# A two-layer block with product-key experts on one core: 32 latent tokens moved from dense expert products to row gathers

## The chip, the core and the metric

One core of a Trainium2 chip. TensorE (PE) multiplies, VectorE (DVE) and ScalarE (ACT) work element by element, GpSimd (POOL) issues the indirect DMAs, SyncE (SP) most other DMAs. The metric is the device time of one execution in microseconds (us).

## The reference, cut to what matters

Two layers, each a mixer followed by `peer` on T = 640 tokens of width D = 1024: 128 context tokens and 512 latent ones, which differ only in their modulation. Each token scores 128 x 128 experts by product keys, takes 16 for each of 8 heads, and mixes their rows:

```python
def peer(h, wq, sub_keys, u, v):
    ...
        eidx = jnp.take_along_axis(cidx, fi, axis=-1)
        g = jax.nn.softmax(fs, axis=-1)
        act = jax.nn.gelu(jnp.einsum('cd,chkd->chk', xc, u[eidx]).astype(F32), approximate=False)
        return jnp.einsum('chk,chkd->cd', (g * act).astype(v.dtype), v[eidx])
```

So a token reads 128 rows of `u` and 128 rows of `v` (4 KB each) of the 16384 in each table.

## The kernel before

**Two ways to the experts.** The 512 latent tokens go through all 16384 experts densely. For each i (128 experts), the product `S` is 24 matmuls of 128x512 (high and low halves of `uT` and of the activations, L1130 to L1133), `S_gelu` takes it through gelu, and `w1` (L1478) multiplies it by the gate matrix `gt`, which is zero for experts that a token did not choose. `w1` also casts the high half `Wh` on ACT, and `w2` (L1486) makes the low half `Wl` on DVE. The output product `O` (L1517 to L1521) sums eight i's at a time: 16 chunks `cc`, in each eight products, one per 128 columns `dt` of D, again 24 matmuls each. `evac` (L1527) adds each into the residual `xT`. The 128 context tokens go by gathers: POOL fetches one row per token (128 rows of 4 KB) by an indirect DMA (L1424). DVE takes its dot product with the activations (`gu`, L1431) or adds it, weighted, to `acc` (`gv`, L1440): 256 such steps per layer. Four row buffers serve them.

**Stages of a layer.** After the mixer come the query projection (`pqs`, L1189) and, tile by tile of 128 tokens, scores (`scp`), the top-k chains on DVE (L1236 on) and transposes of the result (`hk`). Groups of eight tokens get one-hot matrices (DVE, L1338 to L1341), whose products `G` (L1352, L1353) are the gate matrix, stored in `Gd`. During this stage, here the ahead stage, PE also makes 72 of the 128 `S` products (list AHEAD) and stores their gelu in `Sd`; DVE makes the low half `ul` of each `uT` block for them (L220). The main stage follows. In each chunk PE makes the chunk's own `S` products (NMAIN: 3 and 4 in turn), while the chunk's other gelus come back by `reload` (L1491). Then come its eight `O` products, beginning with the reloaded i's.

**What orders the work.** Each engine runs its instructions in the order of the program, in which `step` spreads the ahead products, one-hot groups and rows over the top-k chain. Rows of the main stage are run by `run_items`, one after an `S` (not the first of a chunk) and two after each `O`. Whatever is left after `O` number 5 of the last chunk runs there in one go, ahead of `ctx_end`, whose transposes `aT` bring `acc` into the residual. A reloaded gelu and a new gelu share three buffers (`gep`). A buffer comes free when its `w2` is done:

```python
def w2(pw):
    i, ge, Wh = pw
    ...
    nc.vector.tensor_tensor(Wl, ge, Wh.bitcast(F32), op=OP.subtract)
```

Of the kernel before, what the change touches and what calls it, by code (L numbers as in the profile page):

```python
# [38 lines left out]
NMAIN = [3, 4] * 8  # L39
# [13 lines left out]
def _trunk(ctx, tc, nc, I, O, n_phases):  # L53
# [1051 lines left out]
    def peer(l, last_layer):  # L1105
        with ExitStack() as s:
            Gd = dram.tile([16, P, NI, 32], F32, name=f"Gd{l}")
            Sd = dram.tile([len(AHEAD), P, TS], F32, name=f"Sd{l}")
            hp = s.enter_context(tc.tile_pool(reuse_waits="tile", name=f"ph{l}", bufs=1))
            h2h = hp.tile([P, NC, TS], F32R, name=f"h2h{l}")  # L1110
            h2l = hp.tile([P, NC, TS], F32R, name=f"h2l{l}")
            h2p = hp.tile([P, D], F32, name=f"h2p{l}")
            eidx = hp.tile([P, P], I32, name=f"eidx{l}")
            gp = hp.tile([P, P], F32, name=f"gp{l}")
# [9 lines left out]
            def S_mm(i, w):  # L1124
                hi, lo = w[:2]
                ps = pp.tile([P, TS], F32, name=f"S{l}_{i}", tag="S", bufs=2)

                for c in range(NC + 5):
                    if c < NC:
                        nc.tensor.matmul(ps, hi[:, c], h2h[:, c], start=(c == 0), stop=False)  # L1130
                        nc.tensor.matmul(ps, hi[:, c], h2l[:, c], start=False, stop=False)  # L1131
                    if c >= 5:
                        nc.tensor.matmul(ps, lo[:, c - 5], h2h[:, c - 5], start=False, stop=(c == NC + 5 - 1))  # L1133
                return ps

            def S_gelu(i, ps):
                ge = gep.tile([P, TS], F32, name=f"ge{l}_{i}", tag="ge")
                nc.scalar.activation(ge, ps, AF.Gelu)  # L1138
                return ge
# [3 lines left out]
            def S_ahead():  # L1143
# [6 lines left out]
                n_ahead[0] += 1  # L1150

            with ExitStack() as s2:
# [4 lines left out]
                with ExitStack() as s3:  # L1157
# [10 lines left out]
                    ph32 = php.tile([P, NC, TP], F32, name=f"ph32{l}")  # L1168
# [4 lines left out]
                    for c in range(NC):  # L1173
                        xr = tp.tile([P, T], F32, name=f"pxr{l}_{c}", tag="nt", bufs=3)
                        for tr, a, b in TRUNKS:
# [3 lines left out]
                        nc.scalar.activation(h2h[:, c], xr[:, TP:], AF.Identity, bias=m[:, 1:2])  # L1179
                        nc.scalar.activation(ph32[:, c], xr[:, :TP], AF.Identity, bias=m[:, 0:1])  # L1180
                        nc.vector.scalar_tensor_tensor(h2l[:, c], xr[:, TP:], m[:, 1:2], h2h[:, c].bitcast(F32),
                                                       op0=OP.add, op1=OP.subtract)

                    for n in range(NC):
                        wh, wl, raw = ws.pop(n) if n in ws else wload(wp, I["pwq"][l, n], P, "w")
                        ps = ppn.tile([P, 2, 512], F32, name=f"pqs{l}_{n}", tag="b2")
                        for c in range(NC):
                            for k, (a, b) in enumerate(((wh, h2h), (wl, h2h), (wh, h2l))):
                                nc.tensor.matmul(ps[:, 0, :], a[:, c], b[:, c], start=(c == 0 and k == 0),  # L1189
                                                 stop=(c == NC - 1 and k == 2))  # L1190
# [38 lines left out]
                def topk(tt, sc_, step):  # L1229
                    nm = f"{l}_{tt}"  # L1230
                    sv = tp.tile([P, 16, 16], F32, name=f"sv{nm}", tag="sv")
                    si = tp.tile([P, 16, 16], U32, name=f"si{nm}", tag="si")
# [11 lines left out]
                    cand = tp.tile([P, 8, 112], F32, name=f"cand{nm}", tag="cand", bufs=1)  # L1244
# [11 lines left out]
                    for h in range(8):  # L1256
                        step(17 + h)
                        c2 = tp.tile([P, 112], F32, name=f"c2{nm}_{h}", tag="c2", bufs=2)
# [52 lines left out]
                def to_hk(tt, g, ij):  # L1311
                    ts = slice((tt - 1) * P, tt * P)
                    ps = pk.tile([P, 4, P], F32, name=f"hk{l}_{tt}", tag="sp")
                    nc.tensor.transpose(ps[:, 0], ij[:, 0], ident)
                    nc.tensor.transpose(ps[:, 1], ij[:, 1], ident)
                    nc.tensor.transpose(ps[:, 2], g, ident)
                    nc.scalar.copy(iT[:, ts], ps[:, 0])
                    nc.scalar.copy(jT[:, ts], ps[:, 1])
                    g32 = tp.tile([P, P], F32, name=f"g32{l}_{tt}", tag="g32")
                    nc.scalar.activation(g32, ps[:, 2], AF.Copy, scale=GSC)  # L1320
                    nc.vector.tensor_copy(gh[:, ts], g32)
                    nc.vector.tensor_tensor(gl[:, ts], g32, gh[:, ts], op=OP.subtract)
# [3 lines left out]
                def build(grp):  # L1326

                    ts = slice(grp * 8, (grp + 1) * 8)

                    def bc(t):  # L1330
                        return (t[:, ts].rearrange("p (b t) -> p b t", t=2).unsqueeze(2)
                                .to_broadcast([P, 4, P, 2]))
                    io = iota2.unsqueeze(1).to_broadcast([P, 4, P, 2])
                    oj = ohp.tile([P, 4, P, 2], F16, name=f"oj{l}_{grp}", tag="oj")
                    oi = ohp.tile([P, 4, P, 2], F16, name=f"oi{l}_{grp}", tag="oi", bufs=1)
                    o1 = ohp.tile([P, 4, P, 2], F16, name=f"o1{l}_{grp}", tag="o1")
                    o2 = ohp.tile([P, 4, P, 2], F16, name=f"o2{l}_{grp}", tag="o2")
                    nc.vector.tensor_tensor(oj, bc(jT), io, op=OP.is_equal)  # L1338
                    nc.vector.tensor_tensor(oi, bc(iT), io, op=OP.is_equal)
                    nc.vector.tensor_tensor(o1, oi, bc(gh), op=OP.mult)  # L1340
                    nc.vector.tensor_tensor(o2, oi, bc(gl), op=OP.mult)  # L1341
                    return oj, o1, o2

                def place(grp, oj, o1, o2):
                    if grp % 4 == 0:
                        stg[0] = ohp.tile([P, P, 32], F32, name=f"stg{l}_{grp}", tag="stg")
                    for q in range(2):
                        ps = pk.tile([P, 4, P], F32, name=f"G{l}_{grp}_{q}", tag="G", bufs=4)
                        for r in range(4):
                            t = q * 4 + r  # L1350
                            b, h = t // 2, t % 2
                            nc.tensor.matmul(ps[:, r], oj[:, b, :, h], o1[:, b, :, h], start=True, stop=False)  # L1352
                            nc.tensor.matmul(ps[:, r], oj[:, b, :, h], o2[:, b, :, h], start=False, stop=True)  # L1353
# [3 lines left out]
                    if grp % 4 == 3:  # L1357
                        for a, b in ((0, NI),) if grp < 63 else ((0, 8), (8, NI)):
# [16 lines left out]


                done = 0.0
                for tt in range(NT):
                    share = 0.12 if tt < 2 else 0.195

                    def step(x):
                        ahead_to(done + share * x / 30)
                        while len(todo) > 16 - 16 * x / 30:
                            build_next()
                    sc_ = scores(tt)
                    if tt == 0:
# [4 lines left out]
                    if tt == 0:  # L1391
                        nc.vector.tensor_copy(gp, g)
                        nc.vector.tensor_scalar(ij[:, 0], ij[:, 0], float(P), float(l * NI * P), op0=OP.mult,
                                                op1=OP.add)
                        nc.vector.tensor_tensor(eidx, ij[:, 0], ij[:, 1], op=OP.add)
                        ahead_to(done)
                    else:
# [4 lines left out]
                        todo.extend(range((tt - 1) * 16, tt * 16))  # L1402
# [8 lines left out]
            with ExitStack() as s2:  # L1411
# [7 lines left out]
                eidx2 = rp.tile([P, P], I32, name=f"eidx2{l}", tag="eidx2", bufs=1)
                dots = rp.tile([P, P], F32, name=f"dots{l}", tag="dots", bufs=1)  # L1420

                def gather(table, k, nm):
                    r = rp.tile([P, D], F32, name=f"{nm}{l}_{k}", tag="row")
                    nc.gpsimd.indirect_dma_start(  # L1424
                        out=r[:], out_offset=None, in_=I[table],
                        in_offset=bass.IndirectOffsetOnAxis(ap=eidx2[:, k:k + 1], axis=0))
                    return r

                def ctx_u(k):
                    r = next_row()  # L1430
                    nc.vector.tensor_tensor_reduce(r, r, h2p, 1.0, 0.0, OP.mult, OP.add, dots[:, k:k + 1])  # L1431
# [6 lines left out]
                def ctx_v(k):  # L1438
                    r = next_row()
                    nc.vector.scalar_tensor_tensor(acc, r, dots[:, k:k + 1], acc, op0=OP.mult, op1=OP.add)  # L1440
# [5 lines left out]
                def fetch(n):  # L1446

                    while wanted and len(rows) < n:
                        rows.append(gather(*wanted.pop(0)))
# [5 lines left out]
                for k in range(NI + 16):  # L1455
                    if k < NI:
                        items.append(lambda k=k: ctx_u(k))
                        wanted.append(("pu", k, "gu"))
                    if k % 16 == 15 and k < NI:
                        items.append(lambda k=k: ctx_gate(k - 15, k + 1))  # L1460
                    if k >= 16:
                        items.append(lambda k=k: ctx_v(k - 16))
                        wanted.append(("pv", k - 16, "gv"))
# [5 lines left out]
                def g_load(q):  # L1469
                    if q >= NI // 4:  # L1470
                        return
                    gts[q] = Gp.tile([P, 16, 4, 32], F32, name=f"gt{l}_{q}", tag="gt")
# [3 lines left out]
                def w1(i, ge):  # L1476
                    gv = ge.rearrange("p (g t) -> p g t", g=16)
                    nc.vector.tensor_tensor(gv, gv, gts[i // 4][:, :, i % 4, :], op=OP.mult)  # L1478
                    Wh = wpool.tile([P, TS], F32R, name=f"Wh{l}_{i}", tag="Wh")
# [317 lines left out]
```

## Time and profile before

| | |
|---|---|
| time, median of 3 runs | 4041.17 us (4034.7 to 4048.16) |
| profiled execution | 4047.5 us |
| its span | 4045.7 us |
| PE busy | 3960.8 us, 98% |
| DVE busy | 2952.9 us, 73% |
| ACT, POOL busy | 1556.8 us, 38%; 727.1 us, 18% |
| mean granted TensorE clock | 0.987 |

The span is from the first to the last instruction. Each part of the sum is read from one stage, since the busy shares are means over stages. A matmul's recorded duration overlaps that of the next one; its step is a row's stretch divided by the count of matmuls in it.

### The profile page before, as it was taken

To read this page: it belongs to the slowest core of one execution; us is meant where nothing else is said; L and a number is where in the kernel's file an instruction comes from. 1 tells how busy PE (TensorE), PEld (TensorE's weight loads), DVE (VectorE), ACT (ScalarE), POOL (GpSimd) and SP (SyncE) were. 2 spreads that over 40 slices of the span, in tenths; PEclk is the share of its full clock that TensorE was granted. 3 is DMA by queue.
4 is the path that set the end of the run, shared out by engine and by line. 5 is a ranking of instruction groups with operands and counts; after the bars stand their busy time and mean duration, and the time that the engine had idled before them with its cause. 6 is when DMAs were issued, how large, how long until landed. Compare 5 with 4: busy or idle time off the path is not lost.

```text
span 4045.7 us, 57051 instructions
## 1 busy us (share of the span) xinstructions
PE 3960.8 (98%) x21578; PEld 3257.8 (81%) x21578; DVE 2952.9 (73%) x6091; ACT 1556.8 (38%) x2322; POOL 727.1 (18%) x687
## 2 busy tenths in 40 slices
PE   7999999999999999999999999999999999999998
PEld 5957988888788888888889778888888888888887
DVE  5254469997677777787775664799967787777875
ACT  3334334566323323223343553355663223233231
POOL 0000000000233333333200120000003333333432
PEclk9999999999999999999999999999999999999999
DMA  5152234557888888888552002345578888887884
GB/s 184 59 188 68 84 106 141 195 203 253 276 301 295 275 296 288 293 302 276 209 188 103 22 22 84 113 159 193 199 269 283 273 300 281 294 304 274 295 298 166
DMA packets 363929, 850.80 MB, mean 210 GB/s; under 512 B 27859, under 2 KB 172165, under 8 KB 356869
## 3 DMA queue, kind: packets, MB, share of 16 engines
q1 hardware_dynamic: 289012, 576.04, 41.1%
q0 software_dynamic: 74640, 271.10, 19.2%
q8 instruction: 170, 2.79, 0.3%
q14 instruction: 107, 0.87, 0.1%
HBM read 738.12 MB, written 108.92 MB: 209 GB/s over the span
## 4 chain that ended last, share of the span: by engine, by line
PE 60%; issue 14%; DVE 12%; DMA 7%; POOL 4%; ACT 2%; SPq 0%; POOLq 0%; DVEq 0%; ACTq 0%
PE S L1130 6%; PE S L1131 6%; PE S L1133 6%; PE O L1521 6%; PE O L1517 6%; PE O L1518 6%; PE ow L246 4%; DMA gu<-in_pu_dram,eidx 3%; PE pqs L1189 2%; DMA gv<-in_pv_dram,eidx 2%; POOL gv L1424 2%; POOL gu L1424 2%; PE et L246 2%; DVE ul L220 1%; PE ef L444 1%
## 5 line engine op out<-in xcount | busy, mean ns | idle before, releaser
L1130 PE MATMUL S<-h2h,uh 128*128 128x512 f32 x2048 | 812.3, 397 | 9.3 <-ACT ge L1138 5.6
L1517 PE MATMUL O<-Wh,vh 128*128 128x512 f32 x2048 | 798.1, 390 | 7.1 <-ACT Wh L1480 4.8
L1131 PE MATMUL S<-h2l,uh 128*128 128x512 f32 x2048 | 800.3, 391 | 0.0
L1518 PE MATMUL O<-Wh,vl 128*128 128x512 f32 x2048 | 797.2, 389 | 0.0
L1521 PE MATMUL O<-Wl,vh 128*128 128x512 f32 x2048 | 782.1, 390 | 0.0
L1133 PE MATMUL S<-h2h,ul 128*128 128x512 f32 x2048 | 589.3, 389 | 0.0
L219 ACT CAST vh<-v_raw 128x1024 fp32r<-128x1024 f32 x256 | 269.7, 1053 | 803.9 <-PE O L1521 723.8
L1424 POOL DMA_INDIRECT gv<-in_pv_dram,eidx x256 | 360.8, 1409 | 797.3 <-DVE acc L1440 770.6
L1130 PEld LDWEIGHTS S<-h2h,uh 128*128 128x128 f32 x2048 | 386.1, 189 | 94.5 <-ACT uh L219 7.3
L1517 PEld LDWEIGHTS O<-Wh,vh 128*128 128x128 f32 x2048 | 384.6, 188 | 90.5 <-ACT Wh L1480 7.4
L1521 PEld LDWEIGHTS O<-Wl,vh 128*128 128x128 f32 x2048 | 385.2, 188 | 80.3
L220 DVE TENSOR_TENSOR ul<-u_raw,uh 128x1024 fp32r<-128x1024 f32 x256 | 312.9, 1223 | 186.6 <-ACT uh L219 141.6
L1133 PEld LDWEIGHTS S<-h2h,ul 128*128 128x128 f32 x2048 | 384.5, 188 | 80.0
L1518 PEld LDWEIGHTS O<-Wh,vl 128*128 128x128 f32 x2048 | 384.6, 188 | 79.3
L1131 PEld LDWEIGHTS S<-h2l,uh 128*128 128x128 f32 x2048 | 386.3, 189 | 76.8
L1424 POOL DMA_INDIRECT gu<-in_pu_dram,eidx x256 | 317.7, 1241 | 515.8 <-DVE dots L1431 367.7
L219 ACT CAST uh<-u_raw 128x1024 fp32r<-128x1024 f32 x256 | 269.1, 1051 | 343.2 <-PE S L1131 313.6
L220 DVE TENSOR_TENSOR vl<-v_raw,vh 128x1024 fp32r<-128x1024 f32 x256 | 312.6, 1221 | 110.1 <-ACT vh L219 107.3
L1440 DVE SCALAR_TENSOR_TENSOR acc<-gv,dots,acc 128x1024 f32<-128x1024 f32 x256 | 327.9, 1281 | 42.0 <-DMA gv<-in_pv_dram,eidx 41.2
L1431 DVE CUSTOM_DVE_ANT_0 gu<-gu,h2p 128x1024 f32<-128x1024 f32 x256 | 311.6, 1221 | 54.7 <-DMA gu<-in_pu_dram,eidx 54.6
L1355 ACT ACTIVATE stg<-G 128x512 f32<-128x512 f32 x256 | 260.9, 1159 | 0.7 <-PE G L1353 0.7
L1418 POOL MEMSET acc<- 128x1024 f32 x2 | 1.9, 958 | 1366.2 <-DVE oj L1338 784.9
(399 smaller groups left out, 6003.5 us busy)
## 6 DMA issues: line engine op xcount, KB each, us to landing
u_raw<-in_uT_dram SPq DMA_DIRECT2D x256, 512.0 KB
v_raw<-in_vR_dram SPq DMA_DIRECT2D x256, 512.0 KB
gt<-Gd SPq DMA_DIRECT2D x64, 1024.0 KB
Gd<-stg SPq DMA_DIRECT2D x30, 2048.0 KB
adaw<-in_adaw_dram SPq DMA_DIRECT2D x80, 512.0 KB
Sd<-ge SPq DMA_DIRECT2D x144, 256.0 KB
gr<-Sd SPq DMA_DIRECT2D x134, 256.0 KB
w_raw<-in_ow_dram SPq DMA_DIRECT2D x12, 1024.0 KB
```

The lines of the kernel that those rows point to most:

```text
L219: nc.scalar.copy(hi, raw)
L220: nc.vector.tensor_tensor(lo, raw, hi.bitcast(F32), op=OP.subtract)
L1130: nc.tensor.matmul(ps, hi[:, c], h2h[:, c], start=(c == 0), stop=False)
L1131: nc.tensor.matmul(ps, hi[:, c], h2l[:, c], start=False, stop=False)
L1133: nc.tensor.matmul(ps, lo[:, c - 5], h2h[:, c - 5], start=False, stop=(c == NC + 5 - 1))
L1355: nc.scalar.activation(stg[0][:, :, t0:t0 + 4].rearrange("p i t -> p t i"), ps, AF.Copy, scale=1.0 / GSC)
L1424: nc.gpsimd.indirect_dma_start(out=r[:], out_offset=None, in_=I[table], in_offset=bass.IndirectOffsetOnAxis(ap=eidx2[:, k:k + 1], axis=0))
L1431: nc.vector.tensor_tensor_reduce(r, r, h2p, 1.0, 0.0, OP.mult, OP.add, dots[:, k:k + 1])
L1440: nc.vector.scalar_tensor_tensor(acc, r, dots[:, k:k + 1], acc, op0=OP.mult, op1=OP.add)
L1517: nc.tensor.matmul(ps, hi[:, order[y]], Wh, start=(y == 0), stop=False)
L1518: nc.tensor.matmul(ps, lo[:, order[y]], Wh, start=False, stop=False)
L1521: nc.tensor.matmul(ps, hi[:, x], Ws[n // NC * CH + x][1], start=False, stop=(y == CH + lag - 1))
```

## The change

- XN = 32: the last 32 latent tokens leave the dense part, whose products have ND = 480 columns. Each gathers its 128 rows from each table, four experts of 32 tokens to a gather of 128 rows, so 32 more gathers for `u` and 32 for `v` per layer, with planes of their own in `h2p` and `acc`; `aX`, eight small products, sums the four planes at the end.
- EARLY = 28 context `u` rows are gathered and dotted in the ahead stage, through one buffer (`erow`).
- NMAIN: 40 `S` products in the main stage instead of 56, 88 ahead instead of 72. Seven chunks between the first and the last have 3, the other seven 2; the first has 3, the last 2.
- The top-k tiles go in the order 0, 4, 1, 2, 3. There are 60 one-hot groups instead of 64. Two DVE operations of 128x2048 (`oo`, `og`) replace four of 128x1024.
- The `O` products of dt = 0, 2, 4, 6 stay in four PSUM banks (`OS`) over all chunks and are added to `xT` once; the other `O` have two buffers instead of three.
- `run_items(1)` stands behind every `S` also in a chunk's first.

```diff
-NMAIN = [3, 4] * 8
+XN = 32
+ND = TS - XN
+EARLY = 28
+NMAIN = [3] + [2, 3] * 7 + [2]
...
+            def gather(pool, tag, table, k):
+                r = pool.tile([P, D], F32, name=f"g{table}{l}_{k}", tag=tag, bufs=1 if tag == "erow" else None)
+                nc.gpsimd.indirect_dma_start(
...
+                    nc.vector.tensor_tensor(
+                        og.rearrange("p (q b) v t -> p q b v t", q=2),
+                        oo[:, 4:].unsqueeze(1).to_broadcast([P, 2, 4, P, 2]),
+                        bc(ghl).rearrange("p (q b) v t -> p q b v t", q=2), op=OP.mult)
...
+                def early_to(n):
+
+                    while n_early[0] < min(n, EARLY):
+                        row_dot(early.pop(0) if early else gather(tp, "erow", "pu", 0), n_early[0])
+                        n_early[0] += 1
+                        if n_early[0] < EARLY:
+                            early.append(gather(tp, "erow", "pu", n_early[0]))
...
+                    def step(x):
+                        ahead_to(done + share * x / 30)
+                        if pos:
+                            early_to(round(EARLY * (pos - 1 + x / 30) / (NT - 1)))
...
                 def evac(n, ps):
-                    dt = n % NC
+                    cc, dt = divmod(n, NC)
+                    if dt in pst and cc < NB - 1:
+                        return
...
-                            if x:
-                                run_items(1)
+                            run_items(1)
...
                             if cc or dt > 2:
-                                run_items(2 if dt else 1)
+                                run_items(2)
```

Three places of the order on DVE. The first is where the expert indices of the context tokens (`eidx`) are done and the second tile's top-k is to begin. Before:

```order
L1395 TENSOR_TENSOR eidx_4081<-ij_0_5078 128x128
L220 TENSOR_TENSOR ul_20_5086<-u_20_raw,uh_20_5087 128x1024
L220 TENSOR_TENSOR ul_21_5130<-u_21_raw,uh_21_5131 128x1024
L220 TENSOR_TENSOR ul_22_5210<-u_22_raw,uh_22_5211 128x1024
L220 TENSOR_TENSOR ul_23_5262<-u_23_raw,uh_23_5263 128x1024
L1236 MAX sv_1_5189<-sc_1_5164 128x8 x2
```

Of the change (`gpu` is a gathered row; the row of `dots` below a dot product reads its sum):

```order
L1356 TENSOR_TENSOR eidx_4081<-ec_5221,ij_0_5171 128x128
L224 TENSOR_TENSOR ul_19_5104<-u_19_raw,uh_19_5105 128x1024
L1160 ISA gpu_0_5332,dots_4083<-gpu_0_5332,h2p_4080 128x1024
L1160 ISA dots_4083 128x1
L224 TENSOR_TENSOR ul_20_5179<-u_20_raw,uh_20_5180 128x1024
L1160 ISA gpu_1_5335,dots_4083<-gpu_1_5335,h2p_4080 128x1024
L1160 ISA dots_4083 128x1
L224 TENSOR_TENSOR ul_21_5224<-u_21_raw,uh_21_5225 128x1024
L1160 ISA gpu_2_5430,dots_4083<-gpu_2_5430,h2p_4080 128x1024
L1160 ISA dots_4083 128x1
L224 TENSOR_TENSOR ul_22_5292<-u_22_raw,uh_22_5293 128x1024
L1160 ISA gpu_3_5491,dots_4083<-gpu_3_5491,h2p_4080 128x1024
```

Five dot products (`gpu_0` to `gpu_4`) now stand between the low halves, ahead of the second tile's first MAX; two more such runs, of five and nine, stand in the third and the fourth tile.

The second place is the chunk boundary of chunk 3, before with four reloads (`gr_28` to `gr_31`) and four `S` of its own, now with six and two. Before, from its first `w1`:

```order
L1478 TENSOR_TENSOR gr_28_11295<-gr_28_11295,gt_7_11210 128x512
L1478 TENSOR_TENSOR gr_29_11297<-gr_29_11297,gt_7_11210 128x512
L1486 TENSOR_TENSOR Wl_28_11406<-gr_28_11295,Wh_28_11401 128x512
L1478 TENSOR_TENSOR gr_30_11408<-gr_30_11408,gt_7_11210 128x512
L1486 TENSOR_TENSOR Wl_29_11413<-gr_29_11297,Wh_29_11404 128x512
L1478 TENSOR_TENSOR gr_31_11415<-gr_31_11415,gt_7_11210 128x512
L1486 TENSOR_TENSOR Wl_30_11420<-gr_30_11408,Wh_30_11411 128x512
L1527 SCALAR_TENSOR_TENSOR xT<-O_23_11337,mods_92,xT 128x512
```

Of the change, from the `w2` of the third reload (ahead of it stand `w1` of 26 and 27, `w2` of 26, `w1` of 28, `w2` of 27 and `w1` of 29):

```order
L1549 TENSOR_TENSOR Wl_28_11653<-gr_28_11641,Wh_28_11644 128x480
L1541 TENSOR_TENSOR gr_30_11655<-gr_30_11655,gt_7_11449 128x480
L1549 TENSOR_TENSOR Wl_29_11660<-gr_29_11648,Wh_29_11651 128x480
L1541 TENSOR_TENSOR gr_31_11662<-gr_31_11662,gt_7_11449 128x480
L1549 TENSOR_TENSOR Wl_30_11667<-gr_30_11655,Wh_30_11658 128x480
L1595 SCALAR_TENSOR_TENSOR xT<-O_23_11571,mods_92,xT 128x480
L224 TENSOR_TENSOR ul_32_11672<-u_32_raw,uh_32_11673 128x1024
L1541 TENSOR_TENSOR ge_24_11670<-ge_24_11670,gt_6_11374 128x480
L1549 TENSOR_TENSOR Wl_31_11681<-gr_31_11662,Wh_31_11665 128x480
L1160 ISA gpu_32_11602,dots_4083<-gpu_32_11602,h2p_4080 128x1024
L1160 ISA dots_4083 128x1
L1541 TENSOR_TENSOR ge_25_11711<-ge_25_11711,gt_6_11374 128x480
```

Two reloads were added at the head, two own gelus taken from the tail, and a dot product stands between them; `Wl_24` and `Wl_25`, the last of the chunk, follow.

The third place is the end of the dense part of the first layer. Before:

```order
L1440 SCALAR_TENSOR_TENSOR acc_9945<-gv_127_17372,dots_9948,acc_9945 128x1024
L1527 SCALAR_TENSOR_TENSOR xT<-O_122_17341,mods_92,xT 128x512
L172 TENSOR_TENSOR sq_17266<-sq_17266 128x512
L220 TENSOR_TENSOR vl_126_17439<-v_126_raw,vh_126_17440 128x1024
L1527 SCALAR_TENSOR_TENSOR xT<-O_123_17379,mods_92,xT 128x512
```

Of the change:

```order
L1595 SCALAR_TENSOR_TENSOR xT<-OS_4_10259,mods_92,xT 128x480
L1487 SCALAR_TENSOR_TENSOR acc_10261<-gpv_3_17222,dots_4083,acc_10261 128x1024
L1487 SCALAR_TENSOR_TENSOR acc_10261<-gpv_131_17225,dots_4083,acc_10261 128x1024
L1487 SCALAR_TENSOR_TENSOR acc_10261<-gpv_4_17229,dots_4083,acc_10261 128x1024
L1487 SCALAR_TENSOR_TENSOR acc_10261<-gpv_132_17232,dots_4083,acc_10261 128x1024
L1487 SCALAR_TENSOR_TENSOR acc_10261<-gpv_5_17235,dots_4083,acc_10261 128x1024
```

Eighteen such `acc` rows (to `gpv_139`) now stand behind the addition of `OS_4` and ahead of the ones that take `aT`; before, the last row stood three `O` products ahead of them.

## Rows read from the trace of the kernel before

**Rows 1.** Stages: us, busy us (count) of PE, PEld, DVE, ACT, POOL; clock, DMA, GB/s.

```profile
533.00:1014.00 481.00, 471.19 (x2892) 388.50 (x2892) 439.20 (x1438) 270.09 (x319) 0.96 (x1) 1.00 0.53 188
1014.00:2024.00 1010.00, 1005.11 (x4426) 829.13 (x4426) 777.23 (x980) 305.12 (x395) 340.46 (x256) 1.00 0.81 281
...
3021.00:4035.00 1014.00, 1009.61 (x4438) 832.02 (x4436) 768.90 (x968) 295.62 (x376) 342.87 (x264) 1.00 0.81 280
```

**Rows 2.** Waits of the first main stage: us in all, times, longest.

```profile
PE S L1130 <- ACT uh L219: 1.0, 3, 0.5
```

**Rows 3.** The chain that ended last: start, us, and what; here two runs of matmuls.

```profile
2200.62 8.15 PE ow L246 x68
...
2502.15 5.46 PE pqs L1189 x24
```

**Rows 4.** Instruction groups: busy us, mean ns, idle time before them.

```profile
L1192 PE MATMUL pqs<-ph,w_raw 128*128 128x128 f32 x256 | 31.1, 275 | 0.0
...
L1338 DVE TENSOR_TENSOR oj<-jT,iota 128x1024 f16<-128x1024 f16 x128 | 88.3, 690 | 0.0
...
L1302 DVE TENSOR_TENSOR eq<-eq,sif 128x2048 f16<-128x2048 f16 x20 | 24.9, 1247 | 0.4
...
L1431 DVE CUSTOM_DVE_ANT_0 gu<-gu,h2p 128x1024 f32<-128x1024 f32 x256 | 311.6, 1221 | 54.7 <-DMA gu<-in_pu_dram,eidx 54.6
...
L1440 DVE SCALAR_TENSOR_TENSOR acc<-gv,dots,acc 128x1024 f32<-128x1024 f32 x256 | 327.9, 1281 | 42.0 <-DMA gv<-in_pv_dram,eidx 41.2
```

**Rows 5.** DVE's timeline around a chunk boundary: start, us, idle before in brackets.

```profile
1501.76 1.28 DVE L1440 SCALAR_TENSOR_TENSOR acc<-gv,dots,acc 128x1024 f32<-128x1024 f32 x1
...
1520.36 1.29 DVE L1478 TENSOR_TENSOR gr<-gr,gt 128x512 f32<-128x512 f32 x2
1521.73 0.69 DVE L1486 TENSOR_TENSOR Wl<-gr,Wh 128x512 fp32r<-128x512 f32 x1
1522.35 0.68 DVE L1478 TENSOR_TENSOR gr<-gr,gt 128x512 f32<-128x512 f32 x1
...
1527.10 0.69 DVE L1478 TENSOR_TENSOR gr<-gr,gt 128x512 f32<-128x512 f32 x1 [3.47 <-DMA gr<-Sd]
...
1535.42 1.22 DVE L220 TENSOR_TENSOR ul<-u_raw,uh 128x1024 fp32r<-128x1024 f32 x1 [1.58 <-ACT uh L219]
1536.56 0.68 DVE L1478 TENSOR_TENSOR ge<-ge,gt 128x512 f32<-128x512 f32 x1
```

**Rows 6.** PE's timeline there: the chunk's first product.

```profile
1520.37 0.39 PE L1130 MATMUL S<-h2h,uh 128*128 128x512 f32 x1
```

**Rows 7.** SP's waits from 1200 to 1900 us.

```profile
SPq L1491 <- DVE Wl L1486: 283.9, 17, 24.9
```

**Rows 8.** POOL's timeline at the same boundary.

```profile
1503.30 0.94 POOL L1424 DMA_INDIRECT gv<-in_pv_dram,eidx  x1 [0.65 <-DVE acc L1440]
```

**Rows 9.** DVE's timeline where the context tokens' indices are ready.

```profile
584.40 0.29 DVE L1395 TENSOR_TENSOR eidx<-ij 128x128 int32<-128x128 f32 x1
...
596.37 1.23 DVE L220 TENSOR_TENSOR ul<-u_raw,uh 128x1024 fp32r<-128x1024 f32 x1 [4.21 <-PE S L1133]
598.02 0.49 DVE L1236 MAX8 sv<-sc 128x8 f32<-128x128 f32 x2 [0.42 <-ACT sc L1226]
```

**Rows 10.** Tile hk, all its instructions: min/median/max ns, first and last start.

```profile
L1314 PE MATMUL hk<-ident,ij x8: 272/273/274, 645.4 to 2950.2; 128*128 128x128 f32 x8
```

**Rows 11.** The chain that ended last: a gather's transfer.

```profile
3957.40 6.09 DMA gv<-in_pv_dram,eidx
```

**Rows 12.** POOL's timeline in the last gathers of the second layer.

```profile
3955.24 1.86 POOL L1424 DMA_INDIRECT gv<-in_pv_dram,eidx  x1 [0.66 <-DVE acc L1440]
3957.40 1.85 POOL L1424 DMA_INDIRECT gv<-in_pv_dram,eidx  x1 [0.30 <-issue]
```

**Rows 13.** Short windows, in the output and the top-k phase.

```profile
1360.00:1380.00 20.00, 20.00 (x90) 16.54 (x90) 16.38 (x20) 4.22 (x4) 9.84 (x9) 1.00 1.03 392
600.00:620.00 20.00, 20.00 (x90) 16.53 (x89) 19.97 (x119) 5.34 (x7) 0.00 (x0) 1.00 0.30 101
```

More of the change, by code (lines that the diff above doesn't have):

```diff
@@ L1136, in S_gelu @@
             def S_gelu(i, ps):
-                ge = gep.tile([P, TS], F32, name=f"ge{l}_{i}", tag="ge")
+                ge = gep.tile([P, ND], F32, name=f"ge{l}_{i}", tag="ge")
                 nc.scalar.activation(ge, ps, AF.Gelu)
@@ L1150, in S_ahead, with row_dot @@
                 n_ahead[0] += 1
+            def row_dot(r, k):
+                nc.vector.tensor_tensor_reduce(r, r, h2p[:, int(k >= P)], 1.0, 0.0, OP.mult, OP.add,
+                                               dots[:, k:k + 1])
+            def gather(pool, tag, table, k):
+                r = pool.tile([P, D], F32, name=f"g{table}{l}_{k}", tag=tag, bufs=1 if tag == "erow" else None)
+                nc.gpsimd.indirect_dma_start(
+                    out=r[:], out_offset=None, in_=I[table],
+                    in_offset=bass.IndirectOffsetOnAxis(ap=eidx[:, k:k + 1], axis=0))
+                return r
             with ExitStack() as s2:
@@ L1322, in to_hk, with expert @@
-                    nc.vector.tensor_tensor(gl[:, ts], g32, gh[:, ts], op=OP.subtract)
+                    nc.vector.tensor_copy(ghl[:, gs, 0], by8(g32))
+                    nc.vector.tensor_tensor(ghl[:, gs, 1], by8(g32), ghl[:, gs, 0], op=OP.subtract)
+                def expert(out, ij, nm):
+                    e = tp.tile([P, P], F32, name=f"e{nm}", tag="pab", bufs=1)
+                    nc.vector.tensor_scalar(e, ij[:, 0], float(P), float(l * NI * P), op0=OP.mult, op1=OP.add)
+                    nc.vector.tensor_tensor(out, e, ij[:, 1], op=OP.add)
@@ L1324, in peer, with to_rows @@
+                def to_rows(g, ij):
+                    e = tp.tile([P, P], I32, name=f"ex{l}", tag="sh", bufs=1)
+                    expert(e, ij, f"x{l}")
+                    for r in range(NQ):
+                        rs = slice(r * XN, (r + 1) * XN)
+                        nc.sync.dma_start(eidx[rs, P:], e[P - XN:, rs])
+                        nc.sync.dma_start(gp[rs, P:], g[P - XN:, rs])
                 stg = [None]
                 def build(grp):
-                    ts = slice(grp * 8, (grp + 1) * 8)
@@ L1337, in build @@
[L1337 to L1344, printed above, removed]
+                        return (t[:, grp].rearrange("p q (b t) -> p (q b) t", t=2).unsqueeze(2)
+                                .to_broadcast([P, 8, P, 2]))
@@ L1391, in peer @@
                     if tt == 0:
[L1392 to L1395, printed above, removed]
+                        nc.vector.tensor_copy(gp[:, :P], g)
+                        expert(eidx[:, :P], ij, f"c{l}")
                         ahead_to(done)
@@ L1415, in peer @@
                 rp = s2.enter_context(tc.tile_pool(reuse_waits="tile", name=f"pr{l}", bufs=4))
-                po_ = s2.enter_context(tc.tile_pool(reuse_waits="tile", name=f"ppo{l}", bufs=3, space=PSUM))
-                acc = rp.tile([P, D], F32, name=f"acc{l}", tag="acc", bufs=1)
+                po_ = s2.enter_context(tc.tile_pool(reuse_waits="tile", name=f"ppo{l}", bufs=2, space=PSUM))
+                pst = {dt: po_.tile([P, TS], F32, name=f"OS{l}_{dt}", bufs=1) for dt in range(0, NC, 2)}
+                acc = rp.tile([P, 2, D], F32, name=f"acc{l}", tag="acc", bufs=1)
                 nc.gpsimd.memset(acc, 0.0)
[L1419 to L1431, printed above, removed]
+                sel = rp.tile([P, XN], F32, name=f"sel{l}", tag="sel", bufs=1)
+                nc.vector.tensor_reduce(sel, ident.rearrange("p (r t) -> p t r", t=XN), axis=AX.X, op=OP.add)
                 def ctx_gate(k0, k1):
@@ L1438, in ctx_v @@
                 def ctx_v(k):
-                    r = next_row()
-                    nc.vector.scalar_tensor_tensor(acc, r, dots[:, k:k + 1], acc, op0=OP.mult, op1=OP.add)
+                    a = acc[:, int(k >= P)]
+                    nc.vector.scalar_tensor_tensor(a, next_row(), dots[:, k:k + 1], a, op0=OP.mult, op1=OP.add)
                 items = []
@@ L1448, in fetch @@
                     while wanted and len(rows) < n:
-                        rows.append(gather(*wanted.pop(0)))
+                        rows.append(gather(rp, "row", *wanted.pop(0)))
                 def next_row():
@@ L1510, in out_mm @@
                     hi, lo = vs.pop(n)[:2]
-                    ps = po_.tile([P, TS], F32, name=f"O{l}_{n}", tag="O")
-                    lag = 0 if n % NC else 3
+                    cc, dt = divmod(n, NC)
+                    first, last = (cc == 0, cc == NB - 1) if dt in pst else (True, True)
+                    ps = pst[dt] if dt in pst else po_.tile([P, TS], F32, name=f"O{l}_{n}", tag="O")
+                    ps = ps[:, :ND]
+                    lag = 0 if dt else 3
                     for y in range(CH + lag):
                         if y < CH:
-                            Wh = Ws[n // NC * CH + order[y]][0]
-                            nc.tensor.matmul(ps, hi[:, order[y]], Wh, start=(y == 0), stop=False)
+                            Wh = Ws[cc * CH + order[y]][0]
+                            nc.tensor.matmul(ps, hi[:, order[y]], Wh, start=(first and y == 0), stop=False)
                             nc.tensor.matmul(ps, lo[:, order[y]], Wh, start=False, stop=False)
@@ L1546, in ctx_end @@
                                 op0=OP.mult, op1=OP.add)
+                    ps = po_.tile([P, TS], F32, name=f"aX{l}", tag="O")[:, :NC * XN]
+                    ps = ps.rearrange("p (c t) -> p c t", t=XN)
+                    for c in range(NC):
+                        nc.tensor.matmul(ps[:, c], acc[:, 1, c * P:(c + 1) * P], sel, start=True, stop=True)
+                    for c in range(NC):
+                        nc.vector.scalar_tensor_tensor(
+                            xT[:, c, TP + ND:], ps[:, c], mods[l][:, 5 * NC + c, 1:2], xT[:, c, TP + ND:],
+                            op0=OP.mult, op1=OP.add)
                     if not last_layer:
```

180 lines of the change are left out of this document (109 added, 71 removed).

## The prediction

> **What bounds the kernel now.** I read the table by stages first, then the waits, then the timelines at the places where the order changes.
>
> By stages, TensorE is busy for 471 of 481 us in the ahead stage and for 1005 of 1010 in the main stage of the first layer, 1010 of 1014 in the second [rows 1]. In the main stage its own waits are tiny: 1.0 us behind ScalarE's high half of `u` [rows 2]. So in the main stage each matmul column saved is time saved, as long as its feeders keep up, and the DVE (777 of 1010 us) and the DMA (share 0.81) have some room [rows 1]. The ahead stage is different: inside a top-k chain DVE is busy for 19.97 of 20 us and PE for all 20 [rows 13]. Both are full there, and what is added to either is paid.
>
> Three waits are small now and stand just where the change pushes. At a chunk boundary DVE idles 3.47 us for a reload [rows 5], and SP stood 283.9 us, in 17 waits, for a `Wl` to free a buffer before it could issue a reload [rows 7]. Where the context indices become ready, DVE has nothing to do: it waits 4.21 us for a product [rows 9]. And in the order of before the last `acc` stands three output products ahead of `aT`.
>
> **What the change saves.** A matmul of 512 columns steps at 5.46 / 24 = 227.5 ns, one of 256 columns at 8.15 / 68 = 119.9 [rows 3]. That is 0.420 ns a column, so 480 columns cost 13.45 ns less, 214 in all. An `S` or `O` product of 24 falls from 5.46 to 5.14 us. Dense matmuls: 2 layers x 128 x 24 in S, as many in O, and 192 x 2 in `pqs`: 12672 x 13.45 = **-170 us**. Four one-hot groups less per layer save 8 x 16 matmuls of 128 columns, 54 ns each at the same rate: **-7**. The context projection gets 160 columns instead of 128, at most a quarter of 31.1 us [rows 4]: **+7**. The transposes of `ph4` and `aX`: **+2**. Together **-168**.
>
> What I cost at nothing: the merged one-hots. Two operations of 1247 ns replace four of 690 [rows 4], 0.27 us less per group of busy time, which is about 15 us per layer of DVE at best if nothing overlaps; I take it as 0.1 per group because successive operations overlap by about 0.08 each. If `og`, whose operands are broadcast in another pattern, ran at half rate, 60 groups x 1.2 us would add 72 us per layer to DVE; no row shows that form, and I keep it as a bound only. The 60 evacs that go per layer relieve DVE in the output phase, where it waits for others anyway (16.4 of 20 us busy [rows 13]): 0. The eight banks of PSUM are not a time. With only two buffers left for the odd `O`, which alternate with the `OS`, PE has a whole product of 5.1 us to spare: 0.
>
> **The chunk boundary (+75).** Before, with five reloads, the first product starts at 1520.37 [rows 6]. `w1` of the first two runs at 1520.36, the first `Wl` at 1521.73; it frees its buffer at about 1522.4, and the reload into it is usable at 1527.10 [rows 5]: 4.7 us. Each reload beyond the third starts that late after the `Wl` of the one three before. In the order of the change the `Wl` of the third (28) stands behind `w1` of the fourth (29). So from the boundary: `Wl_26` ends at 2.0; 29 lands at 6.7; `w1` 29 takes 0.6, `Wl_28` ends at 7.9; 31 lands at 12.6. Then DVE does `w1` 31, `Wl_30`, an evac (0.6 each), `ul_32` (1.14, as 1535.42 to 1536.56 [rows 5]), `w1` 24 and `Wl_31` (0.6 each), a dot (1.2), `w1` 25 and `Wl_24` (0.6 each), a short wait for the cast, and `Wl_25`: 6.6 to 7.4, so the last `Wl` is there at about 19.9. PE, with two S products of 5.14, is at the first O at 10.3, and needs `Wl_25` 23 matmuls later, at 15.2. PE idles 4.7 us. With three own S products it needs it at 20.3, and the five reloads end at about the same time: 0. Eight chunks of a layer have two own products (the seven and the last), so 16 x 4.7 = 75. Bounds: 0, if the first `w1` run well before the boundary and the reloads land in 2 us; 16 x 7.5 if each of the two lands as late as a gather does (6.09 [rows 11]).
>
> **The early dots (+92).** One buffer means that a gather can be issued only after the dot before it. VectorE to POOL takes 0.26 us (1501.76 + 1.28 to 1503.30 [rows 5, 8]), the dot 1.22 [rows 4], the gather 6.09 from POOL's start to its landing, the shortest on the chain [rows 11], in a stage with DMA share 0.81; in the ahead stage it is 0.53 [rows 1], so I take 5.5. A cycle is 7.0 us; S products come every 5.14. Where dots stand with only a `ul` (1.14) between them, DVE loses 4.7 us a row.
> - First run, five rows behind `eidx`: from 584.4 [rows 9] to 584.7 + 5 x 7.0 = 620. Before, top-k began at 598.0 [rows 9]; with two more products ahead of the scores it could begin at 602. It is 18 late. PE has 11 products to `hk`, 56.5 us, to 659; top-k took 47.4 us before (598.0 to 645.4 [rows 9, 10]) and gets three `ul` and two dots more, 5.8: it ends at 673. PE idles about 15.
> - Second run: two of its rows (8, 9) stand ahead of the last `ij`, 2 us each of loss, the rest behind it: +10 in two chains.
> - Third run, nine rows, the last of which follow each other closely: about 20 us of loss in a chain that DVE bounds already, since it gets three `ul` (3.4) and nine dots (10.3) more, where PE gets 17 x 5.14 and 16 groups, 101 us. DVE has about 97 + 13 + 15 to 20: +20 or more.
> About 46 us per layer, so the ahead stage, on PE 471 + 16 x 5.14 - 72 x 0.32 = 530, is about 575. Bounds: 0, since DVE waits for PE there before (4.21 us [rows 9]); with 6.09 for the gather, 55.
>
> **The end (+62).** The slots of `run_items` hold 287 of the 301 items; with the gates, 18 rows of `acc` are left ahead of `aT`. Four row buffers with 6.09 + 1.28 + 0.26 give a row every 1.9 us at best [rows 4, 11], and POOL's gathers, when nothing holds them, start 2.16 us apart (3955.24 to 3957.40 [rows 12]). 18 rows take 33 to 39 us, less the first that are already there. The fifth product covers 5.1. PE idles 24 to 34: I take 28, and 3 for `aT` and `aX` taking two buffers in turn. Twice: 62. Lower bound 36, if the gathers are free of the stream and half the rows are there.
>
> **Sum.** -168 + 75 + 92 + 62 = +61. Some of the ahead stage's new idle time covers the 10 us that PE idles per layer there now [rows 1]: -15. So +46 on the profiled execution's 4047.5: 4093; it lies 6 above the median of the runs, so **4088 us**. The main stage would go from 1010 to about 942.
>
> **A rule of the skill.** POOL's issue of a gather took 0.94 us in one row [rows 8] and 1.86 in others [rows 12], with the same form. The Trainium skill, "SBUF — State Buffer", section "SBUF: two separate sides", says that a VectorE operation with two SBUF inputs holds the read port that it shares with GpSimd for the whole instruction, against a GpSimd operation that reads SBUF. The rows fit that, and by the rule a gather issued right behind a dot would wait for the `ul` that starts then; by the 5.5 us taken above the sum is 4088, by the rule 4119, the fourth of the rivals.
>
> **Rivals.**
> - *The early dots cost nothing* (faster). Before, VectorE waits for PE where the first run now stands, and rows that fall into such gaps are free. It holds if a cycle is within an S product, 5.1 us, that is if a gather lands in 3.7. Against it: no gather on the chain took under 6.09. 4088 - 92 = 3996.
> - *Both are cheap*: the reloads also land in time, or DVE begins them before the boundary: 3996 - 40 = 3956.
> - *The boundary costs half* (no change): the first `w1` of a chunk start 2.4 us ahead of it since the evacs are gone: 4088 - 38, 4050, or a little less.
> - *The issue is held*: each closely spaced gather issues in 1.86 instead of 0.94, 0.9 x 17 rows x 2 layers = +31: 4119.
> - *The DMA becomes the bound*: an output product moves 512 KB of `v` and two gathers of 512 KB, with `gt` 1.8 MB in 5.14 us, 355 GB/s; 392 are seen [rows 13]. If the main stage stayed at 281 GB/s [rows 1], it would last 1000 us: 4088 + 116 = 4204.
>
> **How the numbers follow.** About 0.3% (12 us) is what a measurement of this kernel can tell from no change. The forecast, 0.45; early dots free, 0.20; both cheap, 0.07; the boundary at half, 0.12; the issue held, 0.12; DMA, 0.04. Faster 0.27, same 0.12, slower 0.61. The range from 3985 to 4150 leaves out "both cheap" and the DMA, and some of the tails. The forecast's own is 4060 to 4120, by the bounds above.
>
> **What would show it.** S and O products at 5.14 us; PE idle about 4.7 us in the chunks with two own S, in the first O, behind `Wh` or `Wl`, and DVE waiting there twice for reloads; DVE waiting for `gu` between `eidx` and the second tile's first MAX for some 20 us, and PE at `hk` for DVE; a stretch of 30 us with no PE work ahead of `aT`. It is wrong if the ahead stage ends within 540 us, or if the main stages show less than 900.

## The result, and the profile after

The changed kernel takes 4234.6 us (median of 4 runs, 4227.72 to 4243.02), 1.0479 times the time of before (95% interval 1.0452 to 1.0506). The profiled run's span is 4229.8 us, 184.1 longer than before. Its busy times, from the page:

```profile
PE 3915.1 (93%) x21498; PEld 3300.8 (78%) x21498; DVE 2967.7 (70%) x5915; ACT 1538.9 (36%) x2340; POOL 897.8 (21%) x816
```

By stages (columns as in [rows 1]): ahead and main of the first layer, then of the second. The cut at 1116 us lies some 7 us ahead of the first chunk's own products, where [rows 1] cuts; under the experiments the stages are cut at the same instructions in every run.

```profile
524.00:1116.00 592.00, 544.14 (x3181) 463.77 (x3181) 470.35 (x1376) 285.60 (x340) 43.95 (x30) 0.96 0.55 190
1116.00:2104.00 988.00, 908.75 (x4056) 771.12 (x4055) 746.37 (x943) 271.19 (x354) 382.57 (x291) 0.96 0.86 298
2632.00:3224.00 592.00, 541.45 (x3183) 460.23 (x3183) 470.31 (x1376) 285.75 (x341) 43.36 (x30) 0.97 0.55 190
3224.00:4218.00 994.00, 911.06 (x4061) 773.59 (x4060) 745.04 (x939) 267.59 (x347) 385.51 (x299) 0.95 0.86 298
```

The ahead stage went from 481 to 592 us, the main stage from 1010 to 988. In the first layer PE now idles 48 and 79 us of them, where it idled 10 and 5, and its granted clock is 0.96 where it was 1.00.

**The early rows.** DVE's timeline behind `eidx` (a dot product of a gathered row, the low half `ul` that follows it, the next dot), and POOL's (the gathers):

```profile
584.07 1.22 DVE L1160 CUSTOM_DVE_ANT_0 gpu<-gpu,h2p 128x1024 f32<-128x1024 f32 x1 [5.90 <-DMA gpu<-in_pu_dram,eidx]
...
585.22 1.22 DVE L224 TENSOR_TENSOR ul<-u_raw,uh 128x1024 fp32r<-128x1024 f32 x1
592.32 1.23 DVE L1160 CUSTOM_DVE_ANT_0 gpu<-gpu,h2p 128x1024 f32<-128x1024 f32 x1 [5.88 <-DMA gpu<-in_pu_dram,eidx]
...
617.49 1.23 DVE L1160 CUSTOM_DVE_ANT_0 gpu<-gpu,h2p 128x1024 f32<-128x1024 f32 x1 [6.09 <-DMA gpu<-in_pu_dram,eidx]
618.64 0.08 DVE L1160 DVE_READ_ACCUMULATOR2_ANT dots<- 128x1 f32 x1
618.64 0.48 DVE L1259 MAX8 sv<-sc 128x8 f32<-128x128 f32 x2
```
```profile
585.58 1.70 POOL L1165 DMA_INDIRECT gpu<-in_pu_dram,eidx  x1 [6.51 <-DVE dots L1160]
...
610.53 1.68 POOL L1165 DMA_INDIRECT gpu<-in_pu_dram,eidx  x1 [6.78 <-DVE dots L1160]
618.99 0.94 POOL L1165 DMA_INDIRECT gpu<-in_pu_dram,eidx  x1 [6.78 <-DVE sv L1259]
```

A row comes every 8.25 us (584.07 to 592.32), and top-k begins at 618.64. PE stands still meanwhile, and its first matmuls afterwards are slow:

```profile
616.54 0.38 PE L1137 MATMUL S<-h2l,uh 128*128 128x480 f32 x1
627.83 0.77 PE L1139 MATMUL S<-h2h,ul 128*128 128x480 f32 x1 [10.91 <-DVE ul L224]
628.39 0.60 PE L1136 MATMUL S<-h2h,uh 128*128 128x480 f32 x1
...
630.39 2.15 PE L1139 MATMUL S<-h2h,ul 128*128 128x480 f32 x6
632.38 0.38 PE L1136 MATMUL S<-h2h,uh 128*128 128x480 f32 x1
632.60 0.38 PE L1137 MATMUL S<-h2l,uh 128*128 128x480 f32 x1
```

Behind the idle 11 us, 12 matmuls step at about 0.4 us until 632.38, then at 0.22: PE runs at the lower of its two clock levels after the pause (the granted clock is 0.55 from 627.8 to 632.4 us, and 1.00 behind). The 12 take 4.55 us instead of 2.6.

**A boundary with two own products**, on DVE and on PE (columns as in [rows 5, 6]):

```profile
1418.88 0.66 DVE L1549 TENSOR_TENSOR Wl<-gr,Wh 128x480 fp32r<-128x480 f32 x1
...
1426.04 0.66 DVE L1541 TENSOR_TENSOR gr<-gr,gt 128x480 f32<-128x480 f32 x1 [5.36 <-DMA gr<-Sd]
...
1430.04 0.66 DVE L1541 TENSOR_TENSOR gr<-gr,gt 128x480 f32<-128x480 f32 x1 [1.64 <-DMA gr<-Sd]
```
```profile
1431.42 0.49 PE L1583 MATMUL OS<-Wh,vh 128*128 128x480 f32 x1 [1.01 <-ACT Wh L1543]
...
1435.33 0.77 PE L1583 MATMUL OS<-Wh,vh 128*128 128x480 f32 x1 [2.98 <-ACT Wh L1543]
1435.90 0.60 PE L1584 MATMUL OS<-Wh,vl 128*128 128x480 f32 x1
1436.30 0.60 PE L1587 MATMUL OS<-Wl,vh 128*128 128x480 f32 x1
1437.61 0.77 PE L1583 MATMUL OS<-Wh,vh 128*128 128x480 f32 x1 [0.71 <-ACT Wh L1543]
...
1440.92 0.38 PE L1587 MATMUL O<-Wl,vh 128*128 128x480 f32 x1
1441.14 0.37 PE L1583 MATMUL O<-Wh,vh 128*128 128x480 f32 x1
```

DVE waits for the reloaded gelus `gr`, ScalarE's high half `Wh` follows, and PE waits for that: 1.01 + 2.98 + 0.71 = 4.7 us. From 1435.3 to 1440.9 its steps are again 0.4, at a granted clock of 0.50. The page has this wait for all boundaries of both layers, 68.3 us:

```profile
L1583 PE MATMUL OS<-Wh,vh 128*128 128x480 f32 x1024 | 400.5, 391 | 68.4 <-ACT Wh L1543 68.3
```

**The end.** Tile `aT`, what its engine waited for (us, times): the two pauses ahead of the context transposes, one per layer.

```profile
  DVE acc L1487: 72.9, 2
```

### The profile page after: what moved, and what is told of

It reads as the page before. It is cut to its first block, busy times and chain, and to the rows that moved or that the text cites. A ratio compares the mean times of both kernels' runs of the same rounds, so it can differ in the third digit from the quotient of the medians.

```text
span 4229.8 us, 57268 instructions
## 1 busy us (share of the span) xinstructions
PE 3915.1 (93%) x21498; PEld 3300.8 (78%) x21498; DVE 2967.7 (70%) x5915; ACT 1538.9 (36%) x2340; POOL 897.8 (21%) x816
## 4 chain that ended last, share of the span: by engine, by line
PE 40%; issue 21%; DMA 17%; DVE 13%; POOL 7%; ACT 2%; SPq 0%; POOLq 0%; DVEq 0%; ACTq 0%
DMA gpu<-in_pu_dram,eidx 8%; DMA gpv<-in_pv_dram,eidx 5%; PE ow L250 4%; PE S L1136 4%; PE S L1137 4%; PE S L1139 4%; POOL gpu L1165 3%; POOL gpv L1165 3%; PE pqs L1208 2%; DMA gr<-Sd 2%; PE et L250 2%; DVE ul L224 1%; PE ef L448 1%; PE owops L339 1%; PE ewops L339 1%
## 5 line engine op out<-in xcount | busy, mean ns | idle before, releaser
L1136 PE MATMUL S<-h2h,uh 128*128 128x480 f32 x2048 | 796.8, 389 | 23.3 <-ACT uh L223 16.0
L1165 POOL DMA_INDIRECT gpu<-in_pu_dram,eidx x320 | 423.9, 1325 | 1762.2 <-DVE dots L1160 758.4
L1137 PE MATMUL S<-h2l,uh 128*128 128x480 f32 x2048 | 787.5, 385 | 0.0
L1139 PE MATMUL S<-h2h,ul 128*128 128x480 f32 x2048 | 583.4, 387 | 66.0 <-DVE ul L224 66.0
L1165 POOL DMA_INDIRECT gpv<-in_pv_dram,eidx x320 | 422.6, 1321 | 527.9 <-DVE acc L1487 359.9
L1487 DVE SCALAR_TENSOR_TENSOR acc<-gpv,dots,acc 128x1024 f32<-128x1024 f32 x320 | 409.7, 1284 | 92.5 <-DMA gpv<-in_pv_dram,eidx 88.9
L1583 PE MATMUL OS<-Wh,vh 128*128 128x480 f32 x1024 | 400.5, 391 | 68.4 <-ACT Wh L1543 68.3
L1584 PE MATMUL OS<-Wh,vl 128*128 128x480 f32 x1024 | 394.7, 385 | 0.0
L1587 PE MATMUL O<-Wl,vh 128*128 128x480 f32 x1024 | 393.6, 384 | 0.0
L1583 PE MATMUL O<-Wh,vh 128*128 128x480 f32 x1024 | 393.5, 384 | 0.0
```

Source lines behind the costliest of these rows:

```text
L1165: nc.gpsimd.indirect_dma_start(out=r[:], out_offset=None, in_=I[table], in_offset=bass.IndirectOffsetOnAxis(ap=eidx[:, k:k + 1], axis=0))
L1487: nc.vector.scalar_tensor_tensor(a, next_row(), dots[:, k:k + 1], a, op0=OP.mult, op1=OP.add)
L1583: nc.tensor.matmul(ps, hi[:, order[y]], Wh, start=(first and y == 0), stop=False)
L1584: nc.tensor.matmul(ps, lo[:, order[y]], Wh, start=False, stop=False)
L1587: nc.tensor.matmul(ps, hi[:, x], Ws[cc * CH + x][1], start=False, stop=(last and y == CH + lag - 1))
```

## The experiments

Stage lengths below are read from the traces: "ahead" from the first `scp` to the first output matmul, "main" from there to `aT`, first layer. Before: 498 and 980; changed: 615 and 953. Waits and busy times named with them are of the first layer too, if nothing else is said.

**480 columns alone (e1_columns).** The kernel before with

```diff
+ND = 480
-ps = pp.tile([P, TS], F32, name=f"S{l}_{i}", tag="S", bufs=2)
+ps = pp.tile([P, TS], F32, name=f"S{l}_{i}", tag="S", bufs=2)[:, :ND]
```

and the same in the tiles behind it.

> The kernel before with 480 columns in the S and O products, gelu, gate and addition alone (12288 matmuls); the last 32 latent tokens get no expert output, nothing takes its place. Theory: a 480-column matmul steps at about 218 ns on this TensorE, as in the changed kernel's trace, not at the 214 interpolated between 256 and 512 columns, so the saving is 12288 x 9.3 ns = 114 us: 3927 us. Rival: the 218 come from the changed kernel's pauses (its granted clock is 0.96); without them the step is 214, 165 us are saved: 3876 us.

3956.31 us, 0.9791 of before (0.9774 to 0.9807); ahead 486, main 949. At full clock its matmuls step at 218:

```profile
1502.01 0.38 PE L1518 MATMUL O<-Wh,vh 128*128 128x480 f32 x1
...
1504.20 0.38 PE L1519 MATMUL O<-Wh,vl 128*128 128x480 f32 x1
```

Ten steps in 2.19 us. The step is the columns' own; the rival falls. The saving is 87 us, not the 114 of the steps: in the main stage PE idles 8.8 us instead of 3.9, 5.1 of them behind `uh`. The rest of the difference wasn't followed up.

**448 columns (e9_448).** `ND = 448` in the same kernel.

> As the run with 480 columns of the kernel before, with 448: the last 64 latent tokens get no expert output. It measures how a matmul's step depends on its columns: 512 took 227 ns, 480 took 217 to 218, 256 took 120. Theory: from 512 down the step falls by 0.31 ns a column at first: about 208 ns, 6144 x 2 x 19.5 = 240 us less than before in matmul time alone. Rival: only the stretch near 512 is flat, and 448 lies on the line from 256 (0.42 a column): 201 ns, 320 us.

3896.36 us, 0.9632 (0.9605 to 0.9658). O steps:

```profile
1501.64 0.37 PE L1518 MATMUL O<-Wh,vh 128*128 128x448 f32 x1
...
1503.66 0.37 PE L1519 MATMUL O<-Wh,vl 128*128 128x448 f32 x1
```

Ten steps in 2.02 us: the step falls by 0.50 ns a column from 480 to 448, and by 0.31 from 512 to 480. That is close to the rival's 201; the flat stretch is the one next to 512. Of 12288 x 25 ns = 307 us only 149 were gained. A good part of the rest is new idle time: PE stands still for 40.6 us of the main stage instead of 3.9, 34.1 of them behind `uh`. So the matmul time goes as the rival says, and half of what it saves isn't had.

**No early rows (e2_no_early).**

```diff
-                    while n_early[0] < min(n, EARLY):
+                    while False:
```

`dots` is set to zero at the start.

> The changed kernel without the 28 early context rows per layer: neither gathered nor dotted, their dot products taken as zero. Theory: the wait for a single row buffer, and the slow TensorE stretches behind it, make the ahead stage long; from the first scores to the first output product it falls from 614 us to some 545 to 555 in each layer: 4235 - 125 = 4110 us. Rival: VectorE is the bound by its work alone (16 more low halves, one-hots), and only the 28 dots and a part of the waits go: 585 per layer, 4175 us.

4115.56 us, 119 less than the changed kernel. Its first ahead stage:

```profile
535.70:1083.30 547.60, 546.32 (x3286) 471.38 (x3286) 449.39 (x1333) 295.09 (x354) 4.63 (x4) 1.00 0.54 190
```

PE is busy for 546 of 548 us at full clock: without the rows the 88 products bound the stage, and DVE (449) does not. The theory holds; 67 us per layer are the rows' cost. In the changed kernel's 615 us PE is busy for 567, so 47 of the 67 are idle time, and 20 are the longer steps of the same matmuls. Two layers make 134 rather than 119, because the rest of this profile's span is longer: its first `scp` starts at 536 us instead of 524.

**Two early buffers (e10_erow2).**

```diff
-tag=tag, bufs=1 if tag == "erow" else None)
+tag=tag, bufs=2 if tag == "erow" else None)
```

and three raw buffers instead of four for `u` and `v`.

> The changed kernel with two buffers for the early rows, for which the raw u and v blocks get three buffers instead of four. Theory: the single buffer makes the 8.2 us cycle of the early rows; with two the next gather runs under the dot and the row before, and from the first scores to the first output product it takes about 575 us instead of 614: 4235 - 75 = 4160 us. Rival: the gather's own time counts wherever a row stands, since the scheduler puts rows where VectorE has nothing else: 605 us or more, 4215.

4238.46 us, no gain. Ahead falls to 585, between the theory's 575 and the rival's 605: with the second buffer 30 of the 67 us that the rows cost are gone. From 530 to 1040 us DVE still waits 34.0 us for rows instead of 78.0. Main rises to 977, which the missing raw buffer would explain; that part wasn't tried by itself.

**Three more reload buffers (e5_rlbuf).**

```diff
-ge = gep.tile([P, ND], F32, name=f"gr{l}_{i}", tag="ge")
+own = i % CH - NMAIN[i // CH] < 3
+ge = (rlp if own else gep).tile([P, ND], F32, name=f"gr{l}_{i}", tag="ge")
```

> The changed kernel with three more buffers for the first three reloads of a chunk, so that no reload of the six has to wait for a w2. Theory: the idle time behind Wh in the first output product (about 48 us per layer, and some 15 of TensorE at half clock) is the wait for buffers: 4235 - 2 x 50 = 4135 us. Rival: the reloads are late because the transfers are full (0.87 of the DMA engines, against 0.81 before); six at once only land closer together, and the time stays within 20 us: 4215 to 4235.

4119.8 us, 115 less; main 893. Waits from 1100 to 2060 us, of the changed kernel and then of this run:

```profile
DVE gr L1541 <- DMA gr<-Sd: 85.5, 24, 6.0
...
PE OS L1583 <- ACT Wh L1543: 33.6, 22, 3.1
```
```profile
PE OS L1585 <- ACT Wh L1544: 5.3, 6, 1.4
...
PE S L1136 <- ACT uh L223: 0.2, 1, 0.2
```

SP, which waited 355.7 us of the changed kernel's main stage, in 38 waits, for a `Wl` before it could issue a reload, has no such wait left, and the stage's transfers run at 322 GB/s instead of 302. The wait was for buffers, not for bandwidth: the theory holds. Of the 60 us by which the stage got shorter, 28 are PE's wait for `Wh` and 9 its wait for `uh`; 20 are PE's busy time, 855 us instead of 876 for the same matmuls.

**A third row per chunk (e3_spread, e8_rl_spread).**

```diff
-run_items(2)
+run_items(3 if dt == 3 else 2)
```

> The changed kernel with three rows instead of two behind output product 3 of every chunk, so that no rows are left at the end. Theory: the 34 us without TensorE work ahead of the context transposes go, with nothing to pay, since VectorE has room: 4235 - 2 x 32 = 4170 us. Rival: the added gathers make the output phase late, since its transfers run at 0.87 of the DMA engines, and what is saved at the end is lost there: 4225 to 4235 us.

4224.48 us, 10 less, and some of its runs lie among those of the changed kernel. With the reload buffers:

> The same three buffers together with the third row behind output product 3, which by itself gained 10 us instead of 65. Theory: there the loss had moved to the boundaries (S waits for the high half of u, whose load stands behind the reloads in SP's queue); with free buffers SP isn't held, and both gains are had: 4135 - 60 = 4075 us. Rival: the third row takes the transfers' last room, and the gain of the first run alone is all there is: 4125 us or more.

4118.31 us, as without the third row. In both the pauses ahead of `aT` shrink, from 72.9 us in both layers to 9.1 and 12.2, but the main stage is no shorter (954 and 901 us, against 953 and 893 without the third row): PE waits longer for `uh` at the boundaries (same window),

```profile
PE S L1136 <- ACT uh L223: 23.6, 7, 6.4
```
```profile
PE S L1136 <- ACT uh L223: 17.0, 6, 4.1
```

in e3 and e8, against 8.9 in the changed kernel and 0.2 in e5, and its busy time rises by 16 and 14 us for the same matmuls. The theory falls twice: the pause at the end was given back. At the longest of these waits in e8, 4.1 us, it isn't the load of `u` that is late. ACT makes `uh` right behind its other work, with no wait for the load, but that work is four `Wh` (and a gelu):

```profile
1822.15 1.17 ACT L1544 CAST Wh<-gr 128x480 fp32r<-128x480 f32 x2 [12.81 <-DVE gr L1542]
...
1827.31 1.03 ACT L223 CAST uh<-u_raw 128x1024 fp32r<-128x1024 f32 x1
```

The `Wh` wait for DVE, which comes from a series of rows and stood 5.9 us for their gathers from 1801 to 1821. Whether the transfers' bandwidth, as the rival says, or DVE's own time for the added rows makes it late isn't shown.

**The chunks' own products as before (e4_nmain).**

```diff
-NMAIN = [3] + [2, 3] * 7 + [2]
+NMAIN = [3, 4] * 8
```

> The changed kernel with 3 and 4 own S products per chunk, as before (72 ahead). Theory: the reload waits at the boundaries go (some 8 us for each of 16 chunks, half clock included), the ahead stage gets 83 us shorter and the main stage 83 longer per layer, and 16 more slots for rows take away most of the pause at the end: 4235 - 130 - 60 = 4045 us. Rival: the stalls at the boundaries are a matter of bandwidth (the reloads land late whatever their number), and only the pause at the end goes: 4175 us.

4061.23 us, 1.0051 of before (1.0033 to 1.0069); ahead 511, main 970. The theory holds in its causes, with 16 us more than it forecast: PE's wait for `Wh` falls from 33.6 us to 1.3, and the pauses ahead of `aT` to 7.3 in both layers. Left are the early rows (ahead is 511, and 478 without them in the next run) and a wait of 21.8 us for `uh` in the main stage.

**All rows in the main stage (e6_late, e7_late_rl).** As e4, with

```diff
-EARLY = 28
+EARLY = 0
-run_items(2)
+run_items(3 if dt in (2, 5) else 2)
```

and in e7 the reload buffers of e5.

> The changed kernel with 3 and 4 own S products, no early rows (all 128 context rows in the main stage), and three rows behind output products 2 and 5. Theory: the ahead stage falls from 511 us to the matmuls' own 468 in each layer, the main stage pays some 15 for 28 more rows: 4061 - 55 = 4006 us, under the kernel before. Rival: the gathers' transfers bound the main stage, which then grows by 28 rows x 1.7 us, 45 per layer: 4065 us.

4084.38 us, 23 more than e4 and more than either forecast. Ahead is 478, near the theory's 468; main is 1011, 41 longer, near the rival's 45, and S waits 45.9 us for `uh` (from 1100 to 2060 us).

> The run before with the three reload buffers as well. Theory: the 1 to 3 us that S waits for the high half of u at each boundary go with SP's wait for buffers: another 2 x 15, 3975 us. Rival: they are a matter of transfers: no change, 4006 us.

**4000.54 us, 0.9888 of before (0.9867 to 0.991)**: faster than both kernels, by 44 us against the one before. Main is 968, and S waits 20.7 us for `uh`. The buffers gave 84 us, more than the theory's 30, and the rival falls.

## Why the prediction was wrong

The direction and the three losses were right; it gave 4088 us and 4150 at most, 147 and 85 below the measured time. What failed is the size of its terms: the saving came out 50 us too large, the boundary 40 too small, the early dots 27, the end 11. In the boundary and the early dots one thing is missing: the matmuls behind a pause run at the lower clock level, and the prediction priced idle time alone.

- **The saving.** "480 columns cost 13.45 ns less" failed. The line between 256 and 512 columns doesn't hold; the step is 218 ns, and 12672 x 9.5 = 120 us, 50 less than forecast. Not even that was gained by itself: e1, with the `S` and `O` products alone and nothing else changed, gained 87.
- **The boundary.** The idle time was nearly right: 4.7 us in the boundary shown, as forecast, and 68.3 in all on the page (PE behind `Wh`), where the forecast has 75. The price is 115 / 16 = 7.2 (e5). What the prediction left out is the lower clock behind each pause, about 2.5 us in the stretch shown (5.6 us less 0.7 idle, for 11 matmuls of 0.22), and the waits for `uh`.
- **The early dots.** Predicted 92, measured 119 (e2). "46 us per layer" is the idle time, 47, but the slow matmuls bring the cost to 67. That the idle time came out is partly luck: PE idles 18.6, 12.3 and 12.8 us in the three tiles (to 684, 807 and 932 us), where 15, 10 and 20 were forecast, and the cycle is 8.25 us, not 7.0. Of that the rival "the issue is held" has the larger part: POOL's issue takes 1.70 us where a `ul` of two inputs follows the dot (it ends 0.84 us after that `ul`), and 0.94 where the one-input MAX8 does. This agrees with the rule of the Trainium skill ("SBUF — State Buffer", "SBUF: two separate sides"), if a gather's issue counts as an operation that reads SBUF; no run here shows the port itself. That is 0.75 of the 1.25; the rest of the excess is a gather that lands later.
- **The end.** 62 predicted, 72.9 waited. But removing it isn't worth that: without it the main stage was no faster (e3, e8).
- **Nothing**, for the merged one-hots, the fewer evacs and the PSUM banks: `oo` and `og` take 1.22 us each, and in e2 the stage is PE's. The -15 for idle time that is filled was right in size, though the added products fill it: in e2 PE idles 1.3 us of the ahead stage in each layer, before 9.9 and 8.0.

With these sizes the sum is -120 - 7 + 9 + 115 + 119 + 73 - 15 = +174, and the span grew by 184. That they lie close doesn't prove each term: 115 and 119 were taken from kernels that kept the other losses, and with e1's saving the sum would be 33 more.

"Early dots cost nothing", "both are cheap" and "the boundary costs half" fell with e2 and e5. DMA as the bound of the whole stage fell with e5 too, which moves the same bytes in 893 us; its time, 4204, was the nearest of all, by another cause.

## What to carry to other kernels

Price a pause of TensorE by its idle time and the slow matmuls behind it: here about half as much again (20 us beside 37 in e5, 20 beside 47 in e2). Count the buffers along a chain of reloads before shifting work into it; three buffers were worth 115 us. And take a matmul's step from a run at its own size, and expect less than the steps save: shorter products also uncover waits that longer ones hid.

## What was not expected of the hardware

A matmul of 480 columns stepped at 218 ns and one of 448 at 202, beside 227 at 512 and 120 at 256: the steps fall unevenly. After the boundary's pauses of 3 us and less PE ran at the lower clock level for some 5 us, and after one of 11 us no longer; one of 2.84 us, to 885.98, was followed by the full clock. An indirect DMA's issue took 1.7 us beside a two-input operation on DVE, and 0.94 beside a MAX8.
